# A product-key expert layer on one core: half of a dense block moved to gathered experts, and a ScalarE copy ahead of a VectorE product

## The chip, the core and the metric

One NeuronCore of a Trainium2 chip runs the whole program. The metric is the time of one execution in device microseconds.

## The reference, cut to what matters

The model has two layers over 512 latent tokens and 256 context tokens of width 1024, in float32. Each layer mixes tokens, and then runs a product-key expert layer (PEER). The second layer needs no context tokens any more. Per token, 8 heads choose 16 of 16384 experts each:

```python
q = (xb @ wq).reshape(PEER_BLOCK, PEER_HEADS, 2, PEER_DQ)
s = jnp.einsum('thpk,hpnk->thpn', q, subkeys, preferred_element_type=F32)
sv, si = lax.top_k(s, PEER_TOPK)
cand = sv[:, :, 0, :, None] + sv[:, :, 1, None, :]
fv, fi = lax.top_k(cand.reshape(...), PEER_TOPK)
e = jnp.take_along_axis(cidx, fi, axis=-1)
gate = jax.nn.softmax(fv, axis=-1)
act = jax.nn.gelu(jnp.einsum('thkd,td->thk', tab_u[e], xb))
return jnp.einsum('thk,thkd->td', gate * act, tab_v[e])
```

A DeepNorm residual with a layer norm follows. Each token thus has 128 chosen experts, each of them a row of 1024 numbers in `tab_u` and one in `tab_v`.

## The kernel before, in words

Tokens lie in blocks of 128: four latent blocks (0 to 3), two of context (4 and 5). In `layer` the expert layer treats the blocks in two ways. **Dense** blocks (all four latent ones in layer 0, blocks 0 to 2 in layer 1) are run against all 16384 experts, with gates that are zero for those not chosen. **Sparse** blocks (4 and 5 in layer 0, block 3 in layer 1) fetch their chosen rows with indirect DMAs.

*Ahead of the dense stage.* `peer_front` modulates the tokens (`modulate`, L361; where a block is sparse, `to_tokens` also turns it back to token-major in a tile `px`), projects queries, and takes the top 16 of 128 scores per half head. `chosen` (L1385) then finds the 16 best pairs, softmaxes them, and makes either columns of sub-key numbers and gates for one-hot products (given `sT`) or row numbers and gates for gathers (given `e`). For each dense block `build_gates` (L1463) makes, for four tokens at a time, one-hot tiles `ohA` and `ohB` on VectorE, scales `ohB` by the gate on ScalarE (all but the last `bd` of the four, which VectorE scales), multiplies both on TensorE, one 128x128 matmul a token, copies the result to `gsb` and writes it to G in DRAM, as [128 / JB, 128, tokens, JB] with JB = 4 sub-keys side by side. Between these, 26 sub-keys of layer 1 (`early`) get their first product already (`early_pieces`, L1492): a matmul of unsplit float32 over all dense tokens, a GELU, and a store to `ge`. UP sets how far these pieces have gone: 48 per cent before the gates, the rest spread over the steps of the gates.

*The dense stage* (`dense`, L1522) goes over 128 sub-keys. `act(j)` loads 512 KB of `peer_u` (unless the sub-key was early), splits it into two float32r parts (ScalarE rounds, VectorE subtracts; `split`, L107), makes 24 matmuls of 128 x (dense tokens) into `act`, a GELU into `ge`, loads 512 KB of `peer_v`, multiplies `ge` by one of the four sub-keys' gates in `Gt` (L1564, a read with a stride of four numbers), and splits V and W. `out(j, n)` (L1573) then adds W.T V for each dense block n in two halves of 512 columns, three matmuls each (`mm3`, L113), in PSUM banks that stay for the whole stage. In layer 0, where there are four dense blocks and six banks, the fourth goes through `rot` and a VectorE sum.

*The gathers* (`gather`, L1671) run beside it. A sparse block takes 128 steps for U (one indirect DMA of 128 rows, 512 KB, and one VectorE multiply with a sum) and 128 for V (the DMA and one VectorE multiply-add). There are five `gu` buffers. `tick` hands out `rate` steps after each sub-key (half of that after an early one); a gather waits, through `paced`, for a matmul of that moment. The generators lie in `self.bg` and the first one is drained before the second starts. What is left is flushed at sub-key 122, and the sparse blocks are then finished.

The row numbers of a sparse block that isn't in INWIN are made inside the dense stage (`late`, at j == 1): in layer 1 that is `chosen` for block 3.

*The end.* The last four sub-keys' outputs are kept back, and run block by block (L1643 to L1651), each followed by `finish_block`: times the modulation gate, residual, layer norm, store.

Plain DMAs are issued by SP in program order, indirect ones by POOL. The order of instructions on an engine comes from a scheduler that places the program by priorities.

Of the kernel before, what the change touches and what calls it, by code (L numbers as in the profile page):

```python
# [31 lines left out]
JB = 4  # L32
# [2 lines left out]
UG = (((4, 2), (0, 4)), ((4, 2), (0, 4)))  # L35
O4 = 1
ROT = 1
HFO = 1
HK = 5
MG = (((0, 4), (4, 2)), ((0, 3), (3, 1)))  # L40
WQA = 2
# [23 lines left out]
ER = 0.5  # L65
# [25 lines left out]
class Body:  # L91
# [269 lines left out]
    def modulate(self, cols, blocks, h_src, uT, tok=None, pool=None, c0=0, keep=None, ks=range(KC)):  # L361

        nc = self.nc
        n = len(blocks) * 128
        r = 0 if blocks[0] < LB else 1
        late = None
        for k in ks:
            ps = self.ps.tile([128, 512], F, name="mm")
            self.transposes(ps, [h_src[b][:, k * 128:(k + 1) * 128] for b in blocks])
            u = keep[:, k, c0:c0 + n] if keep is not None else pool.tile([128, 512], F, name="uf", bufs=3 if tok else 2)[:, :n]  # L370
            cs = slice(c0, c0 + n)
            mod = dict(scale=cols[0][:, k, r:r + 1], bias=cols[1][:, k, r:r + 1])
# [12 lines left out]
            if tok and blocks[0] in tok:  # L385
                late = lambda k=k, u=u: self.to_tokens(blocks, k, u, tok)
        if late:
            late()

    def to_tokens(self, blocks, k, u, tok):  # L390
        ps = self.ps.tile([128, 512], F, name="mm")
        self.transposes(ps, [u[:, q * 128:(q + 1) * 128] for q in range(len(blocks))])
        for q, b in enumerate(blocks):
            self.nc.scalar.copy(tok[b][:, k * 128:(k + 1) * 128], ps[:, q * 128:(q + 1) * 128])


    def layer(self, l):
# [4 lines left out]
        blocks = lat + cx if need else lat  # L402
        nd = LB if need else LB - 1
        dense, sparse = blocks[:nd], blocks[nd:]
        with ExitStack() as st:
            s_ps = ExitStack()

# [28 lines left out]
            wp.release()  # L436
            kd = self.pool(st, "pk")
            kp = self.pool(st, "gk")
            G = self.dram.tile([128 // JB, 128, nd * 128, JB], F, name=f"G{l}")
            uT = [kd.tile([128, KC, SEQ], R, name=f"u2T{i}") for i in range(2)]  # L440
            with ExitStack() as s2:
                tp = self.pool(s2, "pt", 2)
                slots = [tp.tile([128, 4, 128], F, name=f"pst{i}", bufs=1) for i in range(2)]
                uf = tp.tile([128, KC, nd * 128], F, name="u2", bufs=1)
                top = self.peer_front(l, blocks, dense, sparse, uT, uf, kp, tp, hp)
                self.ge = self.dram.tile([EARLY[l], 128, nd * 128], F, name=f"ge{l}")
                bp = self.pool(s2, "pb", 2)
                self.first_u(l, tp)

                fill = [self.early_pieces(l, i, uf, tp) for i in range(EARLY[l])]  # L450
                if need:
                    k = len(fill)
                    left = range(4 * OC[0] // 16, 4)
                    for i, g in enumerate(left):
                        fill.insert(FIRST + (i + 1) * (k - FIRST) // len(left) + i, self.mod_pieces(l + 1, g, bp, 4, MQ))
                total, steps, done = 8 * len(fill), 128 // GT * nd, UP[l][0]
                fill = self.ahead([x for f in fill for x in f])
                spent = 0

# [6 lines left out]
                    go_on()  # L466
                for n, b in enumerate(dense):
                    sT = slots[n % 2]
                    self.chosen(l, top, b, tp, sT=sT)
                    for _ in self.build_gates(n, sT, G, bp, BD[n], n == nd - 1):  # L470
                        done += UP[l][1] / steps
                        with tc.issue_after(self.last.ins), self.later(3000):
                            go_on()
# [844 lines left out]
    def peer_front(self, l, blocks, dense, sparse, uT, uf, kp, tp, hp):  # L1318
# [1 line left out]
        nc, I = self.nc, self.I  # L1320
        nb = len(blocks)
        n = 128 * nb
        self.x2 = {b: kp.tile([128, D], F, name=f"px{b}") for b in sparse}
        sv = tp.tile([128, NB, 16, 16], F, name="sv", bufs=1)
        si = tp.tile([128, NB, 16, 16], U32, name="si", bufs=1)
        with ExitStack() as s3:
# [58 lines left out]
    def chosen(self, l, top, b, p, e=None, gt=None, sT=None):  # L1385
# [48 lines left out]
        for x, af in enumerate((av, bv)):  # L1434
# [15 lines left out]
                                              t8[:, :, :, wd:2 * wd])  # L1450
                nc.vector.tensor_copy(ov[:, hs], t8[:, :, :, 0])
            ij.append(o)
        if sT is None:
            ef = t
            nc.vector.scalar_tensor_tensor(ef, ij[1], 128.0, ij[0], op0=OP.mult, op1=OP.add)
            nc.vector.tensor_scalar(e, ef, float(l * 16384), None, op0=OP.add)
        else:
            ps = self.ps.tile([128, 4, 128], F, name="mm")
            for c, src in enumerate((ij[0], ij[1], gt)):
                nc.tensor.transpose(ps[:, c, :], src, self.ident)  # L1460
            nc.vector.tensor_copy(sT[:, 0:3, :], ps[:, 0:3, :])

    def build_gates(self, n, sT, G, p, bd, last):  # L1463

        nc = self.nc
        iota = self.iota[:, None, :].to_broadcast([128, GT, 128])
        for t0 in range(0, 128, TG):
            gs = p.tile([128, 128 // JB, TG, JB], F, name="gsb")
            for q in range(0, TG, GT):

# [14 lines left out]
                    nc.scalar.activation(gs[:, :, q + q4:q + q4 + 4, :].rearrange("p b t j -> p t b j"),  # L1485
                                         ps.rearrange("p t (b j) -> p t b j", j=JB), AF.Copy)
                yield
            ends = (0, 1, 128 // JB) if last and t0 + TG == 128 else (0, 128 // JB)
            for a, z in zip(ends, ends[1:]):
                nc.sync.dma_start(G[a:z, :, n * 128 + t0:n * 128 + t0 + TG, :].rearrange("b i t j -> i b t j"), gs[:, a:z])  # L1490

# [30 lines left out]
    def dense(self, l, dense, sparse, uT, G, aps, kd, dp, st, late):  # L1522
# [1 line left out]

        nc, tc, I = self.nc, self.tc, self.I
        nd = len(dense)
        nt = nd * 128
        rest = nd > 3
        rate = len(sparse) * 256 / (GR[l] - ER * EARLY[l])
        acc = []  # L1530
        y4 = kd.tile([128, D], F, name="gy4") if rest else None
        held, groups = {}, []
# [4 lines left out]
        def act(j):  # L1537
# [22 lines left out]
            V = dp.tile([128, D], F, name="dv", bufs=3)  # L1560
            nc.sync.dma_start(V, I['peer_v'][(l * 128 + j) * 128:(l * 128 + j + 1) * 128])
            Vh, Vl = dp.tile([128, D], R, name="dvh", bufs=VB), dp.tile([128, D], R, name="dvl", bufs=VB)
            W = dp.tile([128, nt], F, name="dw")
            nc.vector.tensor_tensor(W, ge, self.Gt[:, :, j % JB], op=OP.mult)  # L1564
            Wh, Wl = dp.tile([128, nt], R, name="dwh", bufs=VB), dp.tile([128, nt], R, name="dwl", bufs=VB)
            self.split(Vh, Vl, V)
            self.split(Wh, Wl, W)
# [5 lines left out]
        def out(j, n, halves=(0, 1)):  # L1573
            W, V = held[j]
            for hf in halves:
                self.last = self.mm3(acc[2 * n + hf], part(W, slice(n * 128, (n + 1) * 128)), part(V, half[hf]), j == 0, j == js[-1])

        def out4(at):
            for _ in out4_halves(at):
# [14 lines left out]
        def finish(b, y):  # L1594
            self.finish_block(l, b, y, tabs, gate, fp, self.h[b], dense if NACT else ())

        for j in range(128):
# [20 lines left out]
            if j == 128 - TAIL - 2:  # L1618
                for s in self.bg:
                    for _ in s:  # L1620
                        pass
                self.bg = []
                self.gp.release()
                self.hn = tc.alloc_tile_pool(name="hn", bufs=1, side="right", reuse_waits="tile")
                fp = self.pool(st, "pf", 2)
                with tc.issue_after(self.last.ins):
                    gate = fp.tile([128, 2, D], F, name="gate", bufs=1)
                    nc.sync.dma_start(gate[:, :1 + self.need], self.bcast(self.gate[l][1][:1 + self.need]))
                    tabs = None
                    if l == DEPTH - 1:  # L1630
                        tabs = fp.tile([128, 2, D], F, name="lnt", bufs=1)
                        nc.sync.dma_start(tabs, self.bcast(I['ln_ffn'][l]))
                    self.h = {}
                    for b in sparse + dense:
                        self.h[b] = self.hn.tile([128, D], F, name=f"hn{b}")
                        nc.sync.dma_start(self.h[b], self.hd[l, 'mid'][b])
                for b in sparse:
                    finish(b, self.y[b])

        if rest:  # L1640
            out4(js)
            finish(dense[3], [y4[:, h] for h in half])
        for n in range(3):  # L1643
            if HFO:
                for hf in range(2):
                    for j in js:
                        out(j, n, (hf,))
            else:
                for j in js:
                    out(j, n)  # L1650
            finish(dense[n], acc[2 * n:2 * n + 2])  # L1651

    def finish_block(self, l, b, y, tabs, gate, p, z, act):
        nc = self.nc
# [15 lines left out]

    def gather(self, l, b, x, e, gt, ys):  # L1671
        nc, I, p = self.nc, self.I, self.gp
        act = p.tile([128, 128], F, name="act")
        for k in range(128):
            t = p.tile([128, D], F, name="gu", bufs=5)
            dma = nc.gpsimd.indirect_dma_start(out=t, out_offset=None, in_=I['peer_u'],  # L1676
                                               in_offset=bass.IndirectOffsetOnAxis(ap=e[:, k:k + 1], axis=0))
            self.paced(dma)
            nc.vector.scalar_tensor_tensor(t, t, 1.0, x, op0=OP.mult, op1=OP.mult, accum_out=act[:, k:k + 1])  # L1679
            yield 1  # L1680
        w = p.tile([128, 128], F, name="gwt")
# [3 lines left out]
        ys[b] = [y[:, :512], y[:, 512:]]  # L1685
        for k in range(128):
# [128 lines left out]
```

## Time and profile before

| | |
|---|---|
| median of 3 runs | 4714.54 us (4711.78 to 4716.38) |
| the profiled execution | 4709.66 us, its span 4707.9 us |
| TensorE (PE) busy | 4500.2 us, 96% |
| VectorE (DVE) busy | 3785.4 us, 80% |
| ScalarE (ACT) busy | 2057.3 us, 44% |
| chain that ended last | PE 68%, DVE 10%, issue 8%, DMA 7%, ACT 5% |
| moved by DMA | 1120.38 MB, mean 238 GB/s |

In the span of 4707.9 us, layer 0's dense stage lies from about 1381 to 2650, layer 1's from about 3708 to the end. Times in rows are us from the span's start unless marked ns; PE is TensorE, PEld its weight loads, DVE VectorE, ACT ScalarE, POOL GpSimd, SP the queue of plain DMAs. Busy time of TensorE counts an instruction from its start to its modelled end, and consecutive matmuls overlap.

### The profile page before, as it was taken

The page shows a single profiled execution, that of the slowest core. Times are in us where ns is not written, and L with a number is a line of the kernel's source. Part 1 is how long each engine was busy: PE and PEld are TensorE (multiplying, and loading weights), DVE is VectorE, ACT ScalarE, POOL GpSimd, SP SyncE. Part 2 cuts the span into 40 slices and gives each one's busy share as a digit, 9 for nine tenths or more (in the row PEclk, how much of TensorE's full clock was granted, in tenths as well). Part 3 has the DMA queues.
Part 4 walks back from the last instruction along what each step waited for, and adds up shares of the span by engine and source line. Part 5 has one row for each costly group of instructions (what it writes and reads, how often), then busy time and mean ns, then how long its engine had stood idle before and what let it go on. Part 6 is the DMA issues. An engine that isn't in the chain of part 4 may idle for free.

```text
span 4707.9 us, 67345 instructions
## 1 busy us (share of the span) xinstructions
PE 4500.2 (96%) x24113; PEld 3811.4 (81%) x24113; DVE 3785.4 (80%) x7649; ACT 2057.3 (44%) x3956; POOL 1073.9 (23%) x772
## 2 busy tenths in 40 slices
PE   7999999999999999999999798898999999999998
PEld 6978888885668888888888697687877888888887
DVE  7857655899989999999999875766698787777777
ACT  4357654225952222222222354665339633333333
POOL 0000000000005555656556200000000044333331
PEclk9999999999999999999999899999999999999999
DMA  7844332623679999999999575543426798888885
GB/s 275 292 143 124 108 98 88 211 71 119 193 240 349 344 346 343 339 355 344 341 343 337 205 282 176 176 144 107 148 90 184 252 350 309 299 298 297 303 297 197
DMA packets 495791, 1120.38 MB, mean 238 GB/s; under 512 B 43312, under 2 KB 244832, under 8 KB 486368
## 3 DMA queue, kind: packets, MB, share of 16 engines
q1 hardware_dynamic: 384864, 713.38, 44.7%
q0 software_dynamic: 110592, 402.70, 23.7%
q8 instruction: 190, 3.11, 0.3%
q14 instruction: 145, 1.19, 0.1%
HBM read 975.14 MB, written 140.80 MB: 237 GB/s over the span
## 4 chain that ended last, share of the span: by engine, by line
PE 68%; DVE 10%; issue 8%; DMA 7%; ACT 5%; POOL 2%; SPq 0%; POOLq 0%; DVEq 0%; ACTq 0%
PE acc L117 5%; PE acc L115 5%; PE act L117 4%; PE acc L116 4%; PE act L115 4%; PE act L116 4%; PE mm L115 3%; PE mm L116 3%; PE mm L117 3%; PE mm L1484 3%; PE sg L115 3%; PE sg L116 3%; PE sg L117 3%; DMA gu<-peer_v,pe 3%; PE S L1506 3%
## 5 line engine op out<-in xcount | busy, mean ns | idle before, releaser
L1676 POOL DMA_INDIRECT gu<-peer_u,pe x384 | 526.4, 1371 | 3023.8 <-DMA dv<-peer_v 1390.7
L1688 POOL DMA_INDIRECT gu<-peer_v,pe x384 | 547.2, 1425 | 539.2 <-PE acc L117 242.3
L115 PE MATMUL act<-u2T,duh 128*128 128x512 f32 (+1 forms) x1656 | 603.2, 364 | 11.7 <-ACT duh L109 11.7
L115 PE MATMUL acc<-dvh,dwh 128*128 128x512 f32 x1536 | 599.8, 391 | 12.3 <-ACT dwh L109 12.2
L117 PE MATMUL act<-u2T,dul 128*128 128x512 f32 (+1 forms) x1656 | 603.3, 364 | 0.4 <-DVE dul L110 0.3
L116 PE MATMUL act<-u2T,duh 128*128 128x512 f32 (+1 forms) x1656 | 602.4, 364 | 0.0
L116 PE MATMUL acc<-dvl,dwh 128*128 128x512 f32 x1536 | 599.5, 390 | 0.0
L1694 DVE SCALAR_TENSOR_TENSOR gy<-gu,gwt,gy 128x1024 f32<-128x1024 f32 x381 | 488.7, 1283 | 116.2 <-DMA gu<-peer_v,pe 111.9
L117 PE MATMUL acc<-dvh,dwl 128*128 128x512 f32 x1536 | 546.4, 391 | 1.6 <-DVE dwl L110 1.4
L1679 DVE SCALAR_TENSOR_TENSOR gu<-gu,px 128x1024 f32<-128x1024 f32 x384 | 462.3, 1221 | 88.8 <-DMA gu<-peer_u,pe 85.6
L109 ACT ACTIVATE dwh<-dw 128x512 fp32r<-128x512 f32 (+1 forms) x256 | 148.2, 579 | 816.0 <-DVE dw L1564 800.1
L109 ACT ACTIVATE dvh<-dv 128x1024 fp32r<-128x1024 f32 x256 | 263.6, 1052 | 335.2 <-PE rot L117 211.2
L109 ACT ACTIVATE duh<-du 128x1024 fp32r<-128x1024 f32 x207 | 218.7, 1057 | 327.1 <-PE act L116 251.5
L115 PEld LDWEIGHTS act<-u2T,duh 128*128 128x128 f32 x1656 | 312.2, 189 | 49.7 <-ACT duh L109 12.5
L115 PEld LDWEIGHTS acc<-dvh,dwh 128*128 128x128 f32 x1536 | 288.3, 188 | 74.6 <-ACT dwh L109 17.6
L116 PEld LDWEIGHTS act<-u2T,duh 128*128 128x128 f32 x1656 | 312.1, 188 | 37.1
L117 PEld LDWEIGHTS acc<-dvh,dwl 128*128 128x128 f32 x1536 | 287.4, 188 | 67.1 <-DVE dwl L110 7.6
L117 PEld LDWEIGHTS act<-u2T,dul 128*128 128x128 f32 x1656 | 311.8, 188 | 36.8 <-DVE dul L110 1.8
L116 PEld LDWEIGHTS acc<-dvl,dwh 128*128 128x128 f32 x1536 | 288.3, 188 | 57.3
L110 DVE TENSOR_TENSOR dvl<-dv,dvh 128x1024 fp32r<-128x1024 f32 x256 | 309.1, 1219 | 27.5 <-ACT dvh L109 24.2
L1506 PE MATMUL S<-u,eu 128*128 128x384 f32 (+1 forms) x752 | 310.1, 536 | 2.8 <-DMA eu<-peer_ut 1.6
L1484 PEld LDWEIGHTS mm<-ohB,ohA 128*128 128x128 f32 x1792 | 233.2, 192 | 97.2 <-ACT ohB L1480 48.6
(394 smaller groups left out, 10728.3 us busy)
## 6 DMA issues: line engine op xcount, KB each, us to landing
dv<-peer_v SPq DMA_DIRECT2D x256, 512.0 KB
du<-peer_ut SPq DMA_DIRECT2D x207, 512.0 KB
G<-gsb SPq DMA_DIRECT2D x26, 2048.0 KB
wmodc<-wmodc SPq DMA_DIRECT2D x84, 512.0 KB
gw<-wgb SPq DMA_DIRECT2D x128, 256.0 KB
Gt<-G SPq DMA_DIRECT2D x31, 1024.0 KB
eu<-peer_ut SPq DMA_DIRECT2D x49, 512.0 KB
Gt<-G SPq DMA_DIRECT2D x31, 768.0 KB
```

Of the source, the lines that this page charges most:

```text
L109: a = self.nc.scalar.activation(hi, src, AF.Copy)
L110: return a, self.nc.vector.tensor_tensor(lo, src, hi, op=OP.subtract)
L115: mm(out, lh, rh, start=first, stop=False)
L116: mm(out, lh, rl, start=False, stop=False)
L117: self.pe = mm(out, ll, rh, start=False, stop=last)
L1484: self.last = nc.tensor.matmul(ps[:, s % 4, :], A[:, s, :], B[:, s, :], start=True, stop=True)
L1506: nc.tensor.matmul(ps[:, :n], U[:, k, :], uf[:, k, :], start=k == 0, stop=k == KC - 1)
L1676: dma = nc.gpsimd.indirect_dma_start(out=t, out_offset=None, in_=I['peer_u'], in_offset=bass.IndirectOffsetOnAxis(ap=e[:, k:k + 1], axis=0))
L1679: nc.vector.scalar_tensor_tensor(t, t, 1.0, x, op0=OP.mult, op1=OP.mult, accum_out=act[:, k:k + 1])
L1688: dma = nc.gpsimd.indirect_dma_start(out=t, out_offset=None, in_=I['peer_v'], in_offset=bass.IndirectOffsetOnAxis(ap=e[:, k:k + 1], axis=0))
L1694: nc.vector.scalar_tensor_tensor(y, t, w[:, k:k + 1], y, op0=OP.mult, op1=OP.add)
```

## The change

In the last layer the third block (block 2) is split in two. Its tokens 0 to 63 stay dense, so all dense tiles have 320 columns in place of 384 (`nt`). Its tokens 64 to 127 are gathered: 64 tokens x 128 experts fill 128 partitions x 64 steps, with partitions 0 to 63 holding a token's first 64 experts and 64 to 127 the same tokens' other 64. `half_to_tokens` puts these tokens into `px`, twice, by transposes, two copies and two DMAs. `chosen` for this block makes both kinds of result, four small DMAs arrange row numbers and gates, and its gather is put into `self.bg` ahead of that of block 3; `rate` rises from 256 to 384 steps in the same number of sub-keys. At the end the two partial sums are added, joined with the dense half, and block 2 is finished ahead of blocks 0 and 1.

In both layers, `act(j)` gets a ScalarE copy of the sub-key's gates out of the strided `Gt` into W, and VectorE multiplies `ge` by W in place.

```diff
@@ modulate
+            elif tok and self.half in blocks and k % 4 == 3:
+                late = lambda k=k: self.half_to_tokens(k, keep[:, :, 128 * self.half + 64:128 * self.half + 128], tok['h'])
+    def half_to_tokens(self, k, u, x):
+        ps = self.ps.tile([128, 512], F, name="mm")
+        self.transposes(ps[:64], [u[:, q, :] for q in range(k - 3, k + 1)])
+        cs = slice((k - 3) * 128, (k + 1) * 128)
+        self.nc.scalar.copy(x[:64, cs], ps[:64])
+        self.nc.sync.dma_start(x[64:, cs], x[:64, cs])
@@ layer
+        self.half = None if need else dense[-1]
+        nt = nd * 128 - (0 if need else 64)
-            G = self.dram.tile([128 // JB, 128, nd * 128, JB], F, name=f"G{l}")
+            G = self.dram.tile([128 // JB, 128, nt, JB], F, name=f"G{l}")
-                fill = [self.early_pieces(l, i, uf, tp) for i in range(EARLY[l])]
+                fill = [self.early_pieces(l, i, uf[:, :, :nt], tp) for i in range(EARLY[l])]
-                total, steps, done = 8 * len(fill), 128 // GT * nd, UP[l][0]
+                total, steps, done = 8 * len(fill), nt // GT, UP[l][0]
-                    self.chosen(l, top, b, tp, sT=sT)
-                    for _ in self.build_gates(n, sT, G, bp, BD[n], n == nd - 1):
+                    own = 128
+                    if b == self.half:
+                        own = 64
+                        e, gt = kp.tile([128, 64], I32, name="peh"), kp.tile([128, 64], F, name="pgh")
+                        ef, gf = tp.tile([128, 128], I32, name="he", bufs=1), tp.tile([128, 128], F, name="hg", bufs=1)
+                        self.chosen(l, top, b, tp, sT=sT, e=ef, gt=gf)
+                        for i in range(2):
+                            for x, f in ((e, ef), (gt, gf)):
+                                nc.sync.dma_start(x[64 * i:64 * i + 64], f[64:, 64 * i:64 * i + 64])
+                        self.bg.append(self.gather(l, 'h', self.x2['h'], e, gt, self.y))
+                    else:
+                        self.chosen(l, top, b, tp, sT=sT)
+                    for _ in self.build_gates(n, sT, G, bp, BD[n], n == nd - 1, own):
@@ build_gates
-        for t0 in range(0, 128, TG):
+        for t0 in range(0, own, TG):
@@ dense
-        nt = nd * 128
+        nt = nd * 128 - (0 if self.half is None else 64)
-        rate = len(sparse) * 256 / (GR[l] - ER * EARLY[l])
+        rate = (len(sparse) + (self.half is not None) / 2) * 256 / (GR[l] - ER * EARLY[l])
             W = dp.tile([128, nt], F, name="dw")
-            nc.vector.tensor_tensor(W, ge, self.Gt[:, :, j % JB], op=OP.mult)
+            nc.scalar.activation(W, self.Gt[:, :, j % JB], AF.Copy)
+            nc.vector.tensor_tensor(W, ge, W, op=OP.mult)
@@ out
-                self.last = self.mm3(acc[2 * n + hf], part(W, slice(n * 128, (n + 1) * 128)), part(V, half[hf]), j == 0, j == js[-1])
+                e = min(nt, n * 128 + 128)
+                self.last = self.mm3(acc[2 * n + hf][:e - n * 128], part(W, slice(n * 128, e)), part(V, half[hf]), j == 0, j == js[-1])
@@ after the flush
+                if self.half is not None:
+                    yh, y = self.gz.tile([128, D], F, name="gyf"), self.y['h']
+                    nc.sync.dma_start(yh[64:], y[:64])
+                    nc.vector.tensor_tensor(yh[64:], yh[64:], y[64:], op=OP.add)
@@ the end
-        for n in range(3):
+        for n in range(3) if self.half is None else (2, 0, 1):
...
+            y = acc[2 * n:2 * n + 2]
+            if dense[n] == self.half:
+                for hf in range(2):
+                    nc.scalar.activation(yh[:64, half[hf]], y[hf][:64], AF.Copy)
+                y = [yh[:, h] for h in half]
+            finish(dense[n], y)
@@ gather
+        n = e.shape[1]
-        for k in range(128):
+        for k in range(n):
```

## Rows read from the trace of the kernel before

**Rows 1.** The page's busy time: engine, us (share of the span), instructions.
```profile
PE 4500.2 (96%) x24113; PEld 3811.4 (81%) x24113; DVE 3785.4 (80%) x7649; ACT 2057.3 (44%) x3956; POOL 1073.9 (23%) x772
```

**Rows 2.** Stretches: sum, busy us of each engine, granted clock, DMA share, GB/s.
```profile
1385.00:2640.00 1255.00, 1252.66 (x5524) 1036.25 (x5524) 1163.52 (x1449) 370.91 (x472) 724.05 (x512) 1.00 0.93 341
3504.00:3655.00 151.00, 146.78 (x789) 109.86 (x787) 125.67 (x381) 125.36 (x355) 0.00 (x0) 1.00 0.59 178
3655.00:3704.00 49.00, 47.59 (x315) 39.76 (x315) 42.99 (x98) 46.04 (x133) 0.00 (x0) 1.00 0.78 225
3708.00:4638.00 930.00, 910.27 (x4485) 810.48 (x4484) 727.53 (x935) 327.69 (x447) 349.60 (x256) 1.00 0.86 305
3760.00:3860.00 100.00, 99.65 (x495) 89.07 (x494) 83.83 (x119) 34.01 (x48) 51.12 (x38) 1.00 0.98 364
```

**Rows 3.** Timeline of TensorE: start us, us, engine, line, operation.
```profile
3708.45 0.63 PE L115 MATMUL act<-u2T,fuh 128*128 128x384 f32 x1
...
4006.17 0.33 PE L115 MATMUL act<-u2T,duh 128*128 128x384 f32 x1
...
4010.01 0.33 PE L116 MATMUL act<-u2T,duh 128*128 128x384 f32 x1
4010.18 0.39 PE L115 MATMUL acc<-dvh,dwh 128*128 128x512 f32 x1
...
4012.26 0.39 PE L116 MATMUL acc<-dvl,dwh 128*128 128x512 f32 x1
```

**Rows 4.** Chain of waits, 3504 to 3712: start us, us, what.
```profile
3587.45 10.23 DMA eu<-peer_ut
...
3681.47 4.46 PE mm L1484 x40
...
3703.75 5.17 PE S L1506 x16
```

**Rows 5.** Groups by form, 3504 to 3704: count, busy us, mean ns, idle before.
```profile
L1506 PE MATMUL S<-u,eu 128*128 128x384 f32 x326 | 117.6, 487 | 2.1 <-ACT ege L1509 1.2 <-DMA eu<-peer_ut 0.8
...
L1484 PE MATMUL mm<-ohB,ohA 128*128 128x128 f32 x768 | 99.3, 277 | 3.6 <-ACT ohB L1480 3.5
```

**Rows 6.** Groups by form, 3708 to 4638, same columns.
```profile
L117 PE MATMUL act<-u2T,dul 128*128 128x384 f32 x772 | 260.4, 337 | 0.3 <-DVE dul L110 0.3
...
L1676 POOL DMA_INDIRECT gu<-peer_u,pe x128 | 177.4, 1386 | 1360.4 <-PE act L117 1144.8 <-PE acc L117 155.3 <-issue 28.8
...
L1694 DVE SCALAR_TENSOR_TENSOR gy<-gu,gwt,gy 128x1024 f32<-128x1024 f32 x125 | 160.4, 1283 | 88.6 <-DMA gu<-peer_v,pe 87.0 <-DVE dw L1564 0.4
L1679 DVE SCALAR_TENSOR_TENSOR gu<-gu,px 128x1024 f32<-128x1024 f32 x128 | 155.5, 1222 | 66.6 <-DMA gu<-peer_u,pe 63.7 <-issue 2.9
...
L1564 DVE TENSOR_TENSOR dw<-ge,Gt 128x384 f32<-128x384 f32 x120 | 101.0, 842 | 5.9 <-DMA ge<-ge 5.9
L110 DVE TENSOR_TENSOR dwl<-dw,dwh 128x384 fp32r<-128x384 f32 x119 | 65.8, 554 | 13.6 <-ACT dwh L109 13.6
L109 ACT ACTIVATE dwh<-dw 128x384 fp32r<-128x384 f32 x120 | 63.0, 525 | 396.0 <-DVE dw L1564 385.9 <-DVE dul L110 8.8 <-issue 1.4
```

**Rows 7.** DMA of 3708 to 4638: totals; queue: packets, MB, share.
```profile
DMA packets 80133, 284.03 MB, mean 305 GB/s; under 512 B 8604, under 2 KB 14532, under 8 KB 79945
...
q0 software_dynamic: 36576, 133.19, 40.5%
```

**Rows 8.** DMA of 3716 to 3732: totals; queue: packets, MB, share.
```profile
DMA packets 1756, 6.40 MB, mean 400 GB/s; under 512 B 194, under 2 KB 322, under 8 KB 1755
...
q1 hardware_dynamic: 1755, 6.39, 101.3%
```

**Rows 9.** Timeline of POOL: first and last gather of layer 1.
```profile
3760.00 0.94 POOL L1676 DMA_INDIRECT gu<-peer_u,pe  x1 [1123.24 <-PE act L117]
...
4636.12 0.94 POOL L1688 DMA_INDIRECT gu<-peer_v,pe  x1 [0.30 <-DVE dw L1564]
```

**Rows 10.** DMA of 3708 to 3760: totals.
```profile
DMA packets 6204, 13.96 MB, mean 268 GB/s; under 512 B 400, under 2 KB 3384, under 8 KB 6201
```

More of the change, by code (lines that the diff above doesn't have):

```diff
@@ L37 @@
 ROT = 1
-HFO = 1
 HK = 5
@@ L445, in layer @@
                 top = self.peer_front(l, blocks, dense, sparse, uT, uf, kp, tp, hp)
-                self.ge = self.dram.tile([EARLY[l], 128, nd * 128], F, name=f"ge{l}")
+                self.ge = self.dram.tile([EARLY[l], 128, nt], F, name=f"ge{l}")
                 bp = self.pool(s2, "pb", 2)
                 self.first_u(l, tp)
-                fill = [self.early_pieces(l, i, uf, tp) for i in range(EARLY[l])]
+                fill = [self.early_pieces(l, i, uf[:, :, :nt], tp) for i in range(EARLY[l])]
                 if need:
@@ L1322, in peer_front @@
         n = 128 * nb
-        self.x2 = {b: kp.tile([128, D], F, name=f"px{b}") for b in sparse}
+        self.x2 = {b: kp.tile([128, D], F, name=f"px{b}") for b in sparse + ['h'] * (self.half is not None)}
         sv = tp.tile([128, NB, 16, 16], F, name="sv", bufs=1)
@@ L1452, in chosen @@
             ij.append(o)
-        if sT is None:
+        if e is not None:
             ef = t
@@ L1456, in chosen @@
             nc.vector.tensor_scalar(e, ef, float(l * 16384), None, op0=OP.add)
-        else:
+        if sT is not None:
             ps = self.ps.tile([128, 4, 128], F, name="mm")
@@ L1461, in chosen, with build_gates @@
             nc.vector.tensor_copy(sT[:, 0:3, :], ps[:, 0:3, :])
-    def build_gates(self, n, sT, G, p, bd, last):
+    def build_gates(self, n, sT, G, p, bd, last, own=128):
         nc = self.nc
         iota = self.iota[:, None, :].to_broadcast([128, GT, 128])
-        for t0 in range(0, 128, TG):
+        for t0 in range(0, own, TG):
             gs = p.tile([128, 128 // JB, TG, JB], F, name="gsb")
@@ L1487, in build_gates @@
                 yield
-            ends = (0, 1, 128 // JB) if last and t0 + TG == 128 else (0, 128 // JB)
+            ends = (0, 1, 128 // JB) if last and t0 + TG == own else (0, 128 // JB)
             for a, z in zip(ends, ends[1:]):
@@ L1642, in dense @@
             finish(dense[3], [y4[:, h] for h in half])
-        for n in range(3):
-            if HFO:
-                for hf in range(2):
[L1646 to L1651, printed above, removed]
+        for n in range(3) if self.half is None else (2, 0, 1):
+            for hf in range(2):
+                for j in js:
+                    out(j, n, (hf,))
+            y = acc[2 * n:2 * n + 2]
+            if dense[n] == self.half:
+                for hf in range(2):
+                    nc.scalar.activation(yh[:64, half[hf]], y[hf][:64], AF.Copy)
+                y = [yh[:, h] for h in half]
+            finish(dense[n], y)
     def finish_block(self, l, b, y, tabs, gate, p, z, act):
@@ L1672, in gather @@
         nc, I, p = self.nc, self.I, self.gp
-        act = p.tile([128, 128], F, name="act")
-        for k in range(128):
+        n = e.shape[1]
+        act = p.tile([128, 128], F, name="act")[:, :n]
+        for k in range(n):
             t = p.tile([128, D], F, name="gu", bufs=5)
@@ L1680, in gather @@
             yield 1
-        w = p.tile([128, 128], F, name="gwt")
+        w = p.tile([128, 128], F, name="gwt")[:, :n]
         nc.scalar.activation(w, act, AF.Gelu_apprx_tanh)
@@ L1684, in gather @@
         y = self.gz.tile([128, D], F, name=f"gy{b}")
-        ys[b] = [y[:, :512], y[:, 512:]]
-        for k in range(128):
+        ys[b] = y if b == 'h' else [y[:, :512], y[:, 512:]]
+        for k in range(n):
             t = p.tile([128, D], F, name="gu", bufs=5)
```

## The prediction

> **What bounds the kernel now.** I read the page's busy shares first [rows 1]: TensorE is busy 96% of the span, VectorE 80%. That mean mixes stages, so the stretches come next [rows 2]. In layer 0's dense stage (1385 to 2640 us) TensorE has no idle time to speak of, 1252.66 of 1255 us, while the DMA engines are at 0.93 and 341 GB/s. In layer 1's dense stage, up to the last gather (3708 to 4638), TensorE is at 910.27 of 930 with DMA at 0.86 and 305 GB/s, VectorE at 727.53. The stretches ahead of it (3504 to 3704, gates and early sub-keys) are TensorE's too: 146.78 of 151 and 47.59 of 49, ScalarE close behind in the second. So every stage that the change touches is TensorE's, and the nearest limit behind it in the dense stages is DMA.
>
> A matmul's price is the distance of two starts, not its busy time, since they overlap: first-product matmuls (act) of 384 columns start 22 in 3.84 us, 0.1745 each; output matmuls (acc) of 512 columns nine in 2.08, 0.231 [rows 3]. That is 0.44 ns a column plus little else, so 320 columns should start every 0.146 us, 0.028 less.
>
> **Part 1, gates and early sub-keys of layer 1.** In 3504 to 3704 TensorE runs 768 gate matmuls at 0.1115 us (40 in 4.46) and 326 early matmuls of 384 columns at 0.323 (16 in 5.17) [rows 4, 5]. The change drops 64 of 384 tokens: 128 of the 768 gate entries, 14.3 us; early ones of 320 columns by proportion 0.269, so 326 x 0.054 = 17.6 us. If TensorE stays the bound, 32 us go. From the other side: ScalarE and VectorE lose only half of the third block's stretch (3655 to 3704: 46.04 and 42.99 us busy of 49 [rows 2]), about 23. I take 27. The early matmuls ahead of 3504 also shrink, but beside top-k work; nothing for them.
>
> **Part 2, what is added ahead of the dense stage.** Eight transposes (0.9 us at the gate matmuls' 0.1115 each), two ScalarE copies of 64x512 (nearest row, 128x384, 0.525 each [rows 6]) and two DMAs onto SP's queue, ahead of the projections' weight loads: at worst 3 us in a row, at best hidden; I take 1.5. The block's `chosen` also makes experts' rows and gates: two VectorE operations, then four small DMAs on SP. SP issues in order, so these wait for `chosen`, and behind them stand loads of early `eu`, G and `ge`. The one such wait in the chain, a late `eu`, cost 10.23 us [rows 4]; so 0 to 10, and I take 1, because `eu` has two buffers and the four DMAs are tiny. Sum of parts 1 and 2: -24.5 us.
>
> **Part 3, layer 1's dense stage.** TensorE: three lines of 772 act matmuls [rows 6], 2316 x 0.028 = 65 us less. The output matmuls don't shrink: the half block has 64 columns of weights, but still 512 moving columns. So TensorE could end the gather stretch in 866 us. VectorE: 64 more u-gathers at 1.222 and 64 more v-gathers at 1.283 [rows 6] add 160 us, 5 more for reading the sums; the product dw has now contiguous operands, so I price it by dwl's row of the same width (0.554, less for 320 columns: 0.49), 120 x 0.35 = 42 less, dwl 8 less. 727.5 + 165 - 50 = 843 us: below layer 0's share (1163.52 of 1255 [rows 2]), which didn't hold TensorE there. POOL: 128 more issues at 1.39 us [rows 6] plus about 0.3 between two, 216 us onto 350 busy; not a bound. ScalarE: 120 copies, between 0.525 (its contiguous row of this width) and 0.842 (what the strided read costs VectorE in dw [rows 6]), some 63 to 101 us in a stretch where it is busy 35%: hidden under its own idle time. In both layers the copy now waits for Gt's load, as VectorE's product did; behind it on ScalarE stand the splits dvh, duh and dwh, for which TensorE waits.
>
> DMA: 284.03 MB moved in the stretch, 133.19 of them gathered [rows 7]. Half as many gathers again are 66.6 MB; Gt and ge shrink by a sixth, about 4.9 MB. 345.7 MB result. At TensorE's 866 us that would be 399 GB/s. This is the unknown on which all rests. Rows: 341 over layer 0's 1255 us, where TensorE and not DMA was the limit (0.93); 364 in the 100 us after the first gathers, share 0.98, gathers and plain loads mixed [rows 2]; 400 with the hardware queue alone, share 101% [rows 8]. Bounds: 345.7/0.341 = 1013 us and 866 us. I take the mixed row, nearest in kind, brought to a full share, 370 GB/s: 934 us, 4 more than the 930 of now. So **the dense stage turns from TensorE's to DMA's, and its 65 us are eaten by the gathers**.
>
> One thing helps and is in that number: today the first gather starts at 3760.00, 52 us after the first dense matmul (3708.45), behind the late `chosen` of the fourth block [rows 3, 9]. The half block's gathers need no late `chosen`, so the full stretch can be used.
>
> **Part 4, the end.** After the last gather (4636.12 [rows 9]) some 108 act matmuls are left (102 sub-keys x 24, less 24 of sub-key 0 and the 2316): -3.0 us; the half block's join (one DMA, one add, two copies) comes before two full blocks and adds under a microsecond. I take -3.
>
> **Part 5, layer 0.** VectorE's product gets cheaper there and ScalarE gets 128 copies, but TensorE idles 2.3 us in 1255 [rows 2]: nothing to win. A copy ahead of a split in ScalarE's order can delay it; ScalarE is busy 371 of 1255 and covers it. Zero, up to +5 if a twentieth of the copies stood bare (128 x 0.842 / 20).
>
> **Sum:** -24.5 + 4 - 3 + 0 = -23.5 on the profiled execution's 4709.66, which is 4686; it lies 4.9 below the median shown (4714.54), so I predict 4691. A measurement of this kernel tells about 0.2%, 9.4 us, from no change.
>
> **The rivals.**
> - *DMA carries less than the row I took, and the kernel is slower.* Place: every sub-key of layer 1's dense stage, where late gathers hold VectorE's in-order queue and with it the splits that TensorE waits for (VectorE waits already 88.6 and 66.6 us there [rows 6]). The sum is zero at 345.7/957.5 = 361 GB/s, 9.4 slower at 357.5. At layer 0's 341 the stretch takes 1013: +83, in all +55, 4770; at 350, 4745. For it: no row longer than 100 us is above 341 in this mix. Against: 341 was all that TensorE asked for, at 0.93. Chance of ending slower 0.28.
> - *DMA is no bound.* TensorE stays in front, 866 us: -64 - 27.5 = -92, 4623. This needs 399 GB/s for 870 us; the mixed rows never show it. 0.05. [...]
> - *The half block's gathers don't start with the stage*, because their indices hang in SP's queue or the copy of tokens is late: the present 52 us stay without them. They carried 13.96 MB [rows 10], of 19.2 that 370 GB/s would: 5.3 MB more to do later, 14 us, so 4705. 0.05.
> - *It just balances* (rates of 357.5 to 364.6): 4705 to 4724, 0.14.
>
> **How the numbers follow.** Forecast (364.6 to 399 GB/s) 0.48. Faster by over 0.2%: 0.48 + 0.05 + half of the third rival, 0.55. Within: 0.14 + the other half, 0.17. Slower: 0.28. The range reaches down to 385 GB/s with 5 us more from part 1 (898 us: -32 - 32.5, about 4650) and up to about 352 (982 us: +52 - 27.5, 4740); the forecast's own range is 4650 to 4705.
>
> **What would show it.** Right: DMA share 0.96 or more and 365 to 375 GB/s from the first dense matmul to the last gather, TensorE near 870 of 934 us with new idle time behind ScalarE's dwh and VectorE's splits, VectorE waiting for `gu` for longer; gates and early stretch near 175 us instead of 200; first gather within 15 us of the first dense matmul; dw at 0.49 us; layer 0 unchanged to 5 us. Wrong: a granted clock under 1.00 in the dense stage (gaps of TensorE long enough to cost it its speed), a DMA share under 0.93 there with TensorE idle too, or a layer 0 stage that is longer.

## The result, and the profile after

| | before | after |
|---|---|---|
| median | 4713.16 us (4 runs, 4708.30 to 4716.38) | 4768.73 us (4 runs, 4763.83 to 4779.23) |
| ratio, 95% interval | | 1.0122 (1.0109 to 1.0136) |
| the profiled execution | 4709.66 us | 4763.83 us, its span 4762.1 us |

The change makes the kernel 1.2% slower; 4691 was predicted, and 4768.73 lies above the range. Three stretches of the two profiled executions say where the time is. They are cut at the first dense matmul and at the start of the last gather, which were 3708.45 and 4636.12 before [rows 3, 9]:

| | before | after | difference | predicted |
|---|---|---|---|---|
| up to the first dense matmul | 3708.45 | 3672.81 | -35.6 | -24.5 |
| from there to the last gather | 927.67 | 1053.57 | +125.9 | +4 |
| from there to the end | 73.54 | 37.45 | -36.1 | -3 |
| sum | 4709.66 | 4763.83 | +54.2 | -23.5 |

The first row below answers to [rows 1]: TensorE falls from 96% to 92% of a longer span. The two timelines after it (TensorE's and POOL's; start, duration, engine, line, operation) give the two ends in the changed kernel; the third is TensorE's last dense matmul before.

```profile
PE 4393.1 (92%) x23993; PEld 3692.7 (78%) x23993; DVE 3817.7 (80%) x7797; ACT 2260.8 (47%) x4153; POOL 1179.4 (25%) x900
```

```profile
3672.81 0.55 PE L114 MATMUL act<-u2T,fuh 128*128 128x320 f32 x1
...
4573.81 0.39 PE L116 MATMUL acc<-dvh,dwl 128*128 128x512 f32 x1
```

```profile
3700.35 0.94 POOL L1710 DMA_INDIRECT gu<-peer_u,peh  x1 [1067.03 <-DMA dv<-peer_v]
...
4726.38 0.94 POOL L1722 DMA_INDIRECT gu<-peer_v,pe  x1 [0.66 <-DVE gy L1728]
```

```profile
4694.00 0.39 PE L117 MATMUL acc<-dvh,dwl 128*128 128x512 f32 x1
```

TensorE's last dense matmul is at 4573.81, 120 us earlier than before. But the gathers go on to 4726. The stretches (columns as in [rows 2]) show the two regimes:

```profile
1385.00:2640.00 1255.00, 1254.94 (x5537) 1039.17 (x5536) 1121.24 (x1449) 511.63 (x599) 682.72 (x512) 1.00 0.93 340
3676.00:4574.00 898.00, 886.93 (x4733) 749.27 (x4732) 732.84 (x1065) 425.90 (x599) 379.67 (x293) 0.99 0.94 337
3800.00:4500.00 700.00, 700.00 (x3741) 590.73 (x3740) 564.73 (x778) 329.92 (x463) 296.58 (x230) 1.00 0.94 337
4574.00:4732.00 158.00, 0.20 (x1) 0.00 (x0) 122.00 (x97) 0.00 (x0) 116.77 (x91) 0.51 0.88 305
```

In the dense stage TensorE is busy 700.00 of 700 us, and DMA stands at 0.94 and 337 GB/s. In these 898 us POOL issues 293 of the 384 gathers. The other 91 run alone from 4574 to 4732, at 1.74 us each (158 / 91), and TensorE does nothing meanwhile. So the stage did not turn from TensorE's to DMA's. It came apart: first TensorE's dense work, then a remnant of gathers.

The groups of VectorE and POOL in 3676 to 4574 (columns as in [rows 5]) tell who waited for whom:

```profile
L1713 DVE SCALAR_TENSOR_TENSOR gu<-gu,px 128x1024 f32<-128x1024 f32 x128 | 154.4, 1217 | 0.0
L1728 DVE SCALAR_TENSOR_TENSOR gyh<-gu,gwt,gyh 128x1024 f32<-128x1024 f32 x63 | 80.6, 1279 | 0.4
L1713 DVE SCALAR_TENSOR_TENSOR gu<-gu,pxh 128x1024 f32<-128x1024 f32 x64 | 77.3, 1221 | 0.0
L1728 DVE SCALAR_TENSOR_TENSOR gy<-gu,gwt,gy 128x1024 f32<-128x1024 f32 x32 | 41.0, 1280 | 0.2
L1590 DVE TENSOR_TENSOR dw<-ge,dw 128x320 f32<-128x320 f32 x128 | 61.0, 484 | 0.0
...
L1589 ACT ACTIVATE dw<-Gt 128x320 f32<-128x320 f32 x128 | 99.0, 781 | 37.7 <-DVE dwl L109 37.1
...
L1710 POOL DMA_INDIRECT gu<-peer_u,pe x128 | 162.6, 1270 | 223.8 <-DVE gu L1713 135.0 <-issue 40.1 <-PE acc L116 21.2
```

Before, VectorE stood idle 88.6 and 66.6 us ahead of these products, nearly all of it for gathered rows [rows 6]. Now it is 0.6 us in all: each gather had landed when its product's turn came. The waiting is on the other side: POOL waits for VectorE's product to free a `gu` buffer. VectorE itself is busy 733 of 898 us, so it had time; 113.3 us it stood idle ahead of `dvl`, for ScalarE's `dvh`. What it lacked was the next gather product at that place in its queue.

VectorE's timeline shows why. Its instructions stand in one order, written when the kernel was made. In the kernel before, none of the 127 multiply-adds of a gathered V row in layer 1 stands behind the split of the last U tile (`dul`):

```profile
4645.75 1.28 DVE L1694 SCALAR_TENSOR_TENSOR gy<-gu,gwt,gy 128x1024 f32<-128x1024 f32 x1
...
4659.67 1.22 DVE L110 TENSOR_TENSOR dul<-du,duh 128x1024 fp32r<-128x1024 f32 x1
```

In the changed kernel 111 of 190 do. These are its last split and its last multiply-add:

```profile
4539.64 1.22 DVE L109 TENSOR_TENSOR dul<-du,duh 128x1024 fp32r<-128x1024 f32 x1
...
4731.82 1.28 DVE L1728 SCALAR_TENSOR_TENSOR gy<-gu,gwt,gy 128x1024 f32<-128x1024 f32 x1 [0.22 <-DMA gu<-peer_v,pe]
```

From that, one theory and two rivals were made:

- **O**: the order written for VectorE holds the gathers back, and DMA is not at its limit.
- **D**: DMA carries no more than about 340 GB/s of this mix, and the order only follows.
- **C**: ScalarE's copy delays the splits.

### The profile page after: what moved, and what is told of

Its sections match the earlier page's. It is cut to its first block, busy times and chain, and to the rows that moved or that the text cites. A ratio compares the mean times of both kernels' runs of the same rounds, so it can differ in the third digit from the quotient of the medians.

```text
span 4762.1 us, 67608 instructions
## 1 busy us (share of the span) xinstructions
PE 4393.1 (92%) x23993; PEld 3692.7 (78%) x23993; DVE 3817.7 (80%) x7797; ACT 2260.8 (47%) x4153; POOL 1179.4 (25%) x900
## 4 chain that ended last, share of the span: by engine, by line
PE 80%; DVE 8%; ACT 6%; DMA 4%; issue 2%; POOL 0%; SPq 0%; DVEq 0%; ACTq 0%; POOLq 0%
PE acc L114 7%; PE acc L115 7%; PE acc L116 7%; PE act L116 7%; PE act L114 7%; PE act L115 7%; PE mm L116 3%; PE mm L115 3%; PE mm L114 3%; PE sg L114 3%; PE sg L115 3%; PE sg L116 3%; DMA gu<-peer_v,pe 2%; PE mm L123 2%; ACT ohB L1504 2%; PE mm L1508 2%
## 5 line engine op out<-in xcount | busy, mean ns | idle before, releaser
L1722 POOL DMA_INDIRECT gu<-peer_v,pe x384 | 509.4, 1327 | 367.5 <-DVE gy L1728 188.2
L115 PE MATMUL acc<-dvl,dwh 128*128 128x512 f32 (+1 forms) x1536 | 599.8, 390 | 0.0
L114 PE MATMUL acc<-dvh,dwh 128*128 128x512 f32 (+1 forms) x1536 | 598.9, 390 | 0.1
L114 PE MATMUL act<-u2T,duh 128*128 128x512 f32 (+1 forms) x1656 | 581.7, 351 | 16.5 <-ACT duh L108 16.5
L115 PE MATMUL act<-u2T,duh 128*128 128x512 f32 (+1 forms) x1656 | 581.2, 351 | 0.0
L116 PE MATMUL acc<-dvh,dwl 128*128 128x512 f32 (+1 forms) x1536 | 532.1, 390 | 0.0
L1710 POOL DMA_INDIRECT gu<-peer_u,peh x64 | 86.1, 1345 | 1170.3 <-DMA dv<-peer_v 1067.0
L1589 ACT ACTIVATE dw<-Gt 128x512 f32<-128x512 f32 (+1 forms) x256 | 244.9, 961 | 240.9 <-DVE dwl L109 238.4
L116 PEld LDWEIGHTS acc<-dvh,dwl 128*128 128x128 f32 (+1 forms) x1536 | 273.7, 179 | 72.7
L115 PEld LDWEIGHTS acc<-dvl,dwh 128*128 128x128 f32 (+1 forms) x1536 | 274.7, 179 | 70.4
L114 PEld LDWEIGHTS acc<-dvh,dwh 128*128 128x128 f32 (+1 forms) x1536 | 274.6, 179 | 66.8 <-ACT dwh L108 0.6
```

The costliest lines, as they stand in the source:

```text
L114: mm(out, lh, rh, start=first, stop=False)
L115: mm(out, lh, rl, start=False, stop=False)
L116: self.pe = mm(out, ll, rh, start=False, stop=last)
L1589: nc.scalar.activation(W, self.Gt[:, :, j % JB], AF.Copy)
```

## The experiments

All ratios are against the kernel before, run on the same chip. "Behind" counts the V multiply-adds of layer 1 that stand behind the last `dul` in VectorE's order.

| run | edit | behind | median us | ratio (95%) |
|---|---|---|---|---|
| after | | 111 | 4768.73 | 1.0122 (1.0109 to 1.0136) |
| e1 | the copy alone | 0 | 4699.14 | 0.9972 (0.9961 to 0.9983) |
| e2 | the half block alone | 110 | 4765.29 | one run |
| e3 | loads wait for gathers | 0 | 4785.64 | 1.0150 (1.0132 to 1.0167) |
| e4 | a quarter of the block | 28 | 4681.71 | 0.9934 (0.9917 to 0.9950) |
| e5 | order tied, four sub-keys back | 0 | 4679.37 | 0.9923 (0.9907 to 0.9940) |
| e6 | e5, half of each V load | 0 | 4636.07 | one run |
| e7 | order tied, eight back | 7 | 4691.53 | one run |
| e8 | e4 with e5's order | 0 | 4668.15 | 0.9902 (0.9885 to 0.9918) |
| e9 | e5 without the copy | 0 | 4693.53 | 0.9958 (0.9945 to 0.9971) |

### e1 and e2: the two halves of the change, each alone

e1 is the kernel before with the copy; e2 is the kernel after without it:

```diff
-            nc.vector.tensor_tensor(W, ge, self.Gt[:, :, j % JB], op=OP.mult)
+            nc.scalar.activation(W, self.Gt[:, :, j % JB], AF.Copy)
+            nc.vector.tensor_tensor(W, ge, W, op=OP.mult)
```

> The kernel before with the ScalarE copy alone, all of block 2 dense. Three theories are on trial. O: the order written for VectorE spaces the gathers' products (111 of the 192 V products of layer 1 stand behind the last split of a U tile in the changed kernel, none in the kernel before), so gathers lag while TensorE runs on, and the rest runs alone at the end. D: the DMA engines carry no more than 340 GB/s of gathers and plain loads together, whatever the order. C: the ScalarE copy ahead of the splits is what delays. O and D: within 0.15% of before, 4713, with layer 0's dense stage unchanged to 3 us. C: 20 us or more above before.

> The changed kernel with VectorE's strided product put back, no ScalarE copy. O and D: within 12 us of the changed kernel's 4769, still some 90 gathers behind the last matmul. C: 25 us or more below it.

e1 gains 0.28% (13 us) where O and D expected nothing. e2 has the whole remnant: its TensorE stops near 4580, its last gather comes at 4727.0, and it takes 4765.29. So C falls: the copy makes no remnant, and without it the remnant stays. The stretches of e2:

```profile
3680.00:4580.00 900.00, 886.97 (x4732) 748.47 (x4730) 763.59 (x1068) 335.69 (x471) 399.79 (x296) 0.99 0.93 337
4580.00:4727.00 147.00, 0.00 (x0) 0.00 (x0) 113.54 (x89) 0.00 (x0) 108.54 (x88) 0.51 0.89 309
```

Where e1's gain lies: the idle time of TensorE ahead of the first output matmul of a set, which waits for the split of W. Two groups of one form, 3708 to 4638 before and 3708 to 4628 in e1:

```profile
L115 PE MATMUL acc<-dvh,dwh 128*128 128x512 f32 x714 | 280.8, 393 | 12.3 <-ACT dwh L109 12.2
```

```profile
L115 PE MATMUL acc<-dvh,dwh 128*128 128x512 f32 x714 | 279.4, 391 | 4.1 <-ACT dwh L109 4.1
...
L1565 DVE TENSOR_TENSOR dw<-ge,dw 128x384 f32<-128x384 f32 x119 | 65.7, 553 | 8.4 <-DMA ge<-ge 8.2
```

The product goes from 842 ns [rows 6] to 553, W is ready earlier, and 8.1 us of TensorE's waiting go. From the first dense matmul to the last gather e1 takes 915.2 us (3710.99 to 4626.16) against 927.7 before, so this is most of the 12.5 us that the stage lost; the rest was not followed.

### e3: every U load waits for a gather product

```diff
-                    nc.sync.dma_start(U, I['peer_ut'][l, j])
+                    dma = nc.sync.dma_start(U, I['peer_ut'][l, j])
+                    if self.half is not None and len(gm) > LAG and gm[-1 - LAG] is not None:
+                        self.after(dma, gm[-1 - LAG], "the loads keep pace with the gathers")
```

`gm` keeps, sub-key by sub-key, the last gather product handed out by then; `LAG` is 3.

> The changed kernel with each load of a U tile of layer 1 held until the gathers handed out three sub-keys earlier are used, so that VectorE's written order has none of the gathers' products behind the last split. The bytes are the same. O: the gathers keep pace, 365 GB/s or more in the dense stage, last gather some 930 us after the first dense matmul, 4680 in all (4660 to 4705). D: 340 GB/s as before, the wait only moves to TensorE, last gather after 1015 us, 4760 (4745 to 4775).

Nothing stands behind the last split now, and the remnant is gone, but the kernel is the slowest of all: 4785.64, above both ranges. By itself it looked like D: 333 GB/s over the stage. A stretch of it, its groups of TensorE (3690 to 4720) and one row of the waits of SP's queue (3800 to 4500; us in all, times, longest) say something else:

```profile
3800.00:4500.00 700.00, 601.39 (x3010) 489.79 (x3008) 552.86 (x731) 270.62 (x373) 340.53 (x262) 0.96 0.90 327
```

```profile
L115 PE MATMUL acc<-dvh,dwh 128*128 128x512 f32 x714 | 302.4, 423 | 89.7 <-ACT dwh L109 85.7 <-issue 2.5 <-ACT dvh L109 1.5
...
L115 PE MATMUL act<-u2T,duh 128*128 128x320 f32 x769 | 243.5, 317 | 38.6 <-ACT duh L109 38.3
```

```profile
SPq L1579 <- DVE gu L1718: 104.7, 37, 9.0
```

The loads were really held, 104.7 us for this gather product alone in 700 us, and all loads stand in SP's one queue behind a held one. DMA's share is down to 0.90, and TensorE, idle 99 of the 700 us, was granted a clock of 0.96 there. The edit changed the order and added a wait at once; it could not tell O from D. What could was the order without a wait: e5.

### e4: a quarter of the block

Tokens 96 to 127 of block 2 are gathered, 0 to 95 stay dense (four partition groups of 32 tokens in place of two of 64):

```diff
-        nt = nd * 128 - (0 if need else 64)
+        nt = nd * 128 - (0 if need else GT_)
...
-                        for i in range(2):
+                        for i in range(GN):
```

> The changed kernel with 32 tokens of block 2 gathered and 96 dense (32 gather steps a table in place of 64, dense tiles of 352 columns). O: 28 of the V products stand behind the last split; TensorE's stretch grows by 34 us, and the end alone shrinks from some 157 us to 40 or 50: 4675 (4655 to 4695). D: 323 MB at 340 GB/s are 950 us, 4695 (4680 to 4710).

4681.71 is faster than both kernels, and lies in O's range and in D's. TensorE is busy 795.14 of 800 us and the last gather (4645.63) is only 12 us behind the last dense matmul (4634.06). DMA moves 339 GB/s. So this run alone does not tell O from D.

```profile
3700.00:4500.00 800.00, 795.14 (x4076) 693.12 (x4075) 655.45 (x921) 380.44 (x516) 333.07 (x263) 1.00 0.93 339
```

### e5, e7: the order alone

VectorE's instructions of `act(j)` are put behind the gather product that was handed out four (e7: eight) sub-keys earlier. This moves instructions in VectorE's own queue; it adds no wait between engines and moves the same bytes. (In the traces POOL's gathers come in the same order as before the tie, but the scheduler also wrote ScalarE's instructions somewhat differently.)

```diff
-            held[i] = act(i)
+            mark = gm[-1 - LAG] if self.half is not None and len(gm) > LAG else None
+            with tc.issue_after(mark.ins) if mark is not None else ExitStack():
+                held[i] = act(i)
```

> The changed kernel with VectorE's order written by hand: its splits of a sub-key of layer 1 stand behind the gathers' products handed out four sub-keys earlier. No wait on a load is added, the bytes are the same, and no gather's product stands behind the last split. O (order alone was at fault; the held loads were what cost the run before): TensorE over 95% busy, 365 GB/s, 4690 (4665 to 4710). D (DMA carries 340 GB/s of this mix): the dense stage at 335 to 345 GB/s with TensorE waiting, VectorE waiting for gu, 4760 (4745 to 4785).

> As e5 with eight sub-keys in place of four (7 V products stand behind the last split). O: as e5 to 10 us. D: as e5, 340 GB/s. If the tie of four sub-keys is itself what costs (VectorE waiting for a late gather holds the next splits), then this run lies 20 us or more below e5.

The stretches of e5, and its first dense matmul, last gather and last dense matmul from the timelines of TensorE and POOL:

```profile
3683.00:4619.00 936.00, 874.49 (x4531) 719.16 (x4532) 825.16 (x1122) 407.89 (x572) 519.62 (x384) 0.99 0.97 369
3800.00:4500.00 700.00, 654.34 (x3401) 537.48 (x3400) 617.72 (x802) 298.77 (x422) 403.67 (x296) 0.99 0.98 371
```

```profile
3671.32 0.55 PE L115 MATMUL act<-u2T,fuh 128*128 128x320 f32 x1
...
4659.66 0.39 PE L117 MATMUL acc<-dvh,dwl 128*128 128x512 f32 x1
```

```profile
4618.88 1.01 POOL L1727 DMA_INDIRECT gu<-peer_v,pe  x1 [0.30 <-issue]
```

All 384 gathers are issued inside the stage, and TensorE gives up 61.5 of 936 us for them. The kernel goes from 1.2% slower to 0.8% faster with nothing changed but the order: 89 us. That shows the written order as the cause of the loss, and D falls with it, since DMA carried 371 GB/s for 700 us. O's time and rate came; its busy share of TensorE, over 95%, did not: it is 93%.

What takes those 61.5 us is not one engine. Three groups of 3683 to 4619:

```profile
L115 PE MATMUL act<-u2T,duh 128*128 128x320 f32 x785 | 248.1, 316 | 46.1 <-ACT ge L1585 34.2 <-ACT duh L109 11.9
...
L1718 DVE SCALAR_TENSOR_TENSOR gu<-gu,px 128x1024 f32<-128x1024 f32 x128 | 153.3, 1218 | 10.3 <-DMA gu<-peer_u,pe 10.1
...
L1715 POOL DMA_INDIRECT gu<-peer_u,pe x128 | 175.3, 1370 | 131.9 <-DVE gu L1718 72.0 <-issue 44.1 <-PE acc L117 8.6
```

TensorE waits for ScalarE's GELU most of all; why that is late was not followed. VectorE stands idle only 21.7 us ahead of its four groups of gather products, against 155.2 ahead of two before, and POOL, over its four groups of gathers, still waits 220 us for VectorE to free `gu` buffers.

e7, where 7 multiply-adds are left behind, ends its gathers at 4651.7 and takes 12 us more than e5, 2 over what was expected; it is one run, and the six of e9 alone lie within 12 us. It is not 20 us faster, as was expected if holding VectorE's splits to four sub-keys were itself what costs.

### e6: e5 with fewer bytes

Only the first half of each V tile of layer 1 is loaded and split twice, 33.5 MB less:

```diff
-            nc.sync.dma_start(V, I['peer_v'][(l * 128 + j) * 128:(l * 128 + j + 1) * 128])
...
+            nc.sync.dma_start(V[:, :512] if less else V, I['peer_v'][(l * 128 + j) * 128:(l * 128 + j + 1) * 128, :512 if less else D])
...
+                self.split(Vh.rearrange("p (a b) -> p a b", a=2), Vl.rearrange("p (a b) -> p a b", a=2),
+                           V[:, None, :512].to_broadcast([128, 2, 512]))
```

> The run e5 with half of each V tile of layer 1 loaded (512 columns, split twice, so that the second half of every output row repeats the first half's weights; all instruction sizes but the load are kept). 33.5 MB less. O: as e5, within 15 us, since DMA is not what holds. D: 33.5 MB at 340 GB/s are 98 us: the gathers' stretch becomes 918 us, 4665 (4645 to 4690).

43 us less than e5, where O had expected 15 at most and D 98 (its 4665 was counted from a slower e5). 33.5 MB at 371 GB/s would be 90 us. The stage itself, from the first dense matmul to the last gather, takes 893.7 us (3680.27 to 4574.00) against 947.6 in e5 (3671.32 to 4618.88): 54 us less. The first dense matmul came 9 us later, where the edit changes nothing. In the row below TensorE's busy time in the same 700 us rises from 654.34 to 684.55 while DMA stays at 0.97. So the bytes are a part of what holds e5's stage, and by this one run somewhat more than half of their time came back; DMA alone does not set it.

```profile
3800.00:4500.00 700.00, 684.55 (x3614) 568.59 (x3614) 652.42 (x848) 320.79 (x451) 452.12 (x312) 1.00 0.97 359
```

### e8, e9: what is best, and the copy once more

e8 is e4 with e5's tie; e9 is e5 with the strided VectorE product in place of copy and contiguous product. Their edits are those shown above.

> A quarter of the block gathered (32 tokens, 96 dense) and VectorE's order tied as in e5 (the products of the dense stage's sub-keys stand behind the gather products four sub-keys back). In e4 TensorE was busy 946.59 of the 952 us from 3683 to 4635, so this stage is TensorE's with or without the tie, and the order is worth only what was left behind the last matmul: e4's last gather came at 4645.6, some 10 us after TensorE's last matmul, and e4 took 4681.7. O (the written order spaced the gathers, DMA is no bound here): 4673, between 4662 and 4685. D (DMA carries no more than 340 GB/s of this mix): 312 MB or so go in 920 us at 340 GB/s, so it would not show; the same 4673 to 4690. If the tie itself costs TensorE time through VectorE's queue (as waits in e3 did), 4690 or more, with TensorE under 95 of each 100 us.

> e5 without the ScalarE copy: the strided VectorE product (727 ns in e2 at 320 tokens against 489 ns in e5) and VectorE's order tied as in e5. 128 products of layer 1 cost VectorE about 0.24 us more each, 30 us in the dense stage: 825 + 30 = 855 us busy of 936. If VectorE is covered (DMA and TensorE set the stage): 4680 to 4695, within 15 us of e5's 4679 (e1's copy alone was worth 13 us, whose place was in the dense stage). If VectorE is what sets e5's stage, as the one engine that both gathers and splits go through: 30 us later, 4705 to 4715. Against the kernel before both stay under 4715; the half block alone is then worth 0 to 35 us once the order is right.

e8 takes 4668.15, 0.98% under the kernel before and the lowest median but for e6, which leaves loads out (its interval overlaps e5's). It is where it was expected, but not quite by the expected way: the gathers now end at 4606.14 and the last dense matmul comes at 4652.56, 18 us later than in e4. So the tie costs TensorE 18 us, and the end behind the gathers gives back more. In e4 37 us of the span lie behind the last gather (4645.63 to 4682.8), in e8 only 17 behind the last matmul (4652.56 to 4669.5). Both pay ahead of the stage: their first dense matmuls come at 3699.78 and 3699.34, 28 us after e5's.

```profile
3800.00:4500.00 700.00, 689.29 (x3517) 595.11 (x3516) 582.93 (x753) 319.86 (x439) 372.49 (x254) 1.00 0.94 347
```

e9 is 14 us above e5, as much as e1's copy gained in the kernel before (13). That is the upper edge of the first expectation, and under half of the 30 us by which VectorE's product is longer: VectorE alone does not set the stage, but it is not covered either. The profiled execution of e9, 4703.11, is the slowest of its six; in it the stage from the first dense matmul to the last gather takes 12.6 us more than in e5 (960.15 against 947.56). Of these, 5.8 show as TensorE's wait for the split of W (ahead of the output matmuls 18.8 us in e9, 13.0 in e5); the rest was not followed.

## Why the prediction was wrong

**The step that failed is part 3's step from rates to a common end**, with the first rival's reason for it: "late gathers hold VectorE's in-order queue and with it the splits that TensorE waits for". Both took it that a gather which is late stops TensorE, so that gathers and sub-keys end together and the slower of the two resources sets the time. That needs the gather products to stand among the sub-keys' splits over the whole stage. In the kernel before they did. In the changed kernel 111 of 190 stood behind the last U split. TensorE then never waited for a gather (it was busy 886.93 of the stage's 898 us, and 700.00 of 700 in its middle), and 91 gathers were left over. The price: 190.0 us from the last dense matmul to the end (4573.81 to 4763.83) in place of 15.7 (4694.00 to 4709.66). That TensorE ended 120.2 us earlier pays for so much of these 174.3, and 54 remain.

**The slower rival has the right time and the wrong mechanism.** It gave 4770 at 341 GB/s; the kernel runs at 337 and takes 4768.73. But 337 was what the order asked for, not what DMA could carry: e5 carries 371 over the same 700 us. The agreement is a coincidence, and only e5 shows it.

**The resource figures of part 3 were right.** With the order mended, the stage is the one that was computed: 344.92 MB at 369 GB/s in 936 us for 345.7 at 370 in 934, and TensorE 874 us busy for 870. e5 takes 4679.37, within the 4650 to 4705 of the forecast. That the stage turns from TensorE's to DMA's is borne out only in part, even there: the forecast had VectorE waiting longer for `gu`, and it stands idle for it 21.7 us against 155.2; and of the 90 us that e6's bytes are worth, 54 came back. The prices of matmuls held too: in the changed kernel those of 320 columns start every 0.146 us, and the half block's output matmuls, with 64 columns of weights, every 0.23 like the full ones (4200 to 4206).

**Parts 1 and 2** were 11 us too careful: the first dense matmul came 35.6 us earlier, not 24.5, the bound by TensorE (32) and a little over. In e3, e5, e6 and e7, whose edits begin only there, it lies between 3671.32 and 3680.27, so some 28 to 37 us earlier. Some of it is lost at once: in the first 28 us of the stage TensorE idles 11 us (16.93 busy of 3676 to 3704; before 22.18 of 3708 to 3736), 10.5 of it for the first `duh`. A granted clock under 1.00 was named as a sign of being wrong. It is found in these 28 us alone, 0.76 (0.88 before): behind a gap of 10.5 us the first-product matmuls start every 0.27 us (3689.14 to 3689.94), ahead of it every 0.146 (3673.20 to 3676.42); from 3704 to 4574 the clock is 1.00, so this is not what failed.

```profile
3676.00:3704.00 28.00, 16.93 (x81) 14.81 (x81) 18.02 (x53) 14.28 (x19) 2.98 (x3) 0.76 1.00 361
```

**Part 4**: after the last gather 36.1 us less, not 3, since no dense matmul is left there; it belongs to the failed step. In e5, 11.9.

**Part 5** held: TensorE 1254.94 of 1255 in layer 0.

**The third rival** came half true: the first gather is at 3700.35, 27.5 us behind the first dense matmul (15 were allowed, 52 before). By the order above it had no weight: the gathers lacked places later, not time at the start. No run shows that apart.

**The copy** was priced well in its parts (0.484 us for the product, 0.49 predicted; 0.781 for ScalarE, between 0.525 and 0.842), but its worth was put at nothing. The 842 ns of the strided product lay on the path from `ge` to W that TensorE waited for, 12.2 us in the row before. `Gt` is read four float32 numbers apart, and in the traces such reads took longer: 842 ns (before) against 553 for the same product from contiguous data (e1), and on ScalarE 781 for the strided copy against 467 for `dwh` of the same size (after). What in the read costs this time was not shown.

What stays open: why the scheduler put the products so far back when half a block more was gathered. The program hands them out evenly, sub-key by sub-key; that its priorities let the splits pass is the likely reason, and was not tried apart from the ties. Open too is what sets the stage once the order is right: e6 says in part DMA, e9 in part VectorE.

## What to carry to other kernels

When background work shares an engine with the main path, read where its instructions stand in that engine's written order before using rates: here a stage that DMA could carry (371 GB/s in e5, 337 asked for) still left 91 of 384 gathers, as the order spaced them too thinly. Two signs gave it away: VectorE hardly waited for the data (0.6 us), and the rest of the work ran alone at the end (158 us). That the data's issuer waits for the engine to free buffers is not enough: POOL does so in the mended e5 too, 220 us. Tie the order, not the loads: putting the main path's instructions behind earlier background ones was worth 89 us here, while a wait on the load queue lost 17.

## What was not expected of the hardware

- Gathers and plain loads together ran at 371 GB/s and a share of 0.98 for 700 us (e5). At 337 GB/s the share was 0.94 already (after, 3800 to 4500): 10% more came with a share only 0.04 higher, so a share of 0.94 did not mean that DMA was at its limit. Gathers alone, with five buffers, ran at 305 GB/s and 0.88 (after, 4574 to 4732).
- When TensorE had stopped at 4574, the granted clock was 0.51 (after, 4574 to 4732). It cost nothing there, as no dense matmul was left.
- 0.28% came from a copy that adds 1020 ns of ScalarE's time on average to each of 256 sub-keys (page of e1), and takes 0.29 us off VectorE's in layer 1: the detour was cheap here, where the engine that took it had time (ScalarE busy 327.69 of 930 us before [rows 2]) and the product that got shorter stood on the path (8.1 us less of TensorE's waiting).
